# A hybrid decoder trunk on one Trainium2 core: its recurrence laid as one scheduling region, with a head's steps laid singly, POOL taking part of the DVE work, and the out weights split while the last head runs

## The chip, the cores and the metric

The kernel runs on one core of a Trainium2 chip. The core has a matrix engine (TensorE, here PE, with its weight loads as PEld), a vector engine (VectorE, DVE), an activation engine (ScalarE, ACT), a general engine (GpSimd, POOL) and an engine that only issues transfers here (SyncE, SP). Each runs its own instructions in the order in which they are laid, and waits for the others by semaphores. SBUF is the on-chip memory of 128 partitions; PSUM is the memory that matmuls write. The metric is the device time of one launch in microseconds.

## What is computed

The trunk has two layers on 1024 tokens of width 1024, all in fp32. Layer 0 mixes tokens with a gated linear recurrence, layer 1 with sliding-window attention; each layer has a gated FFN with a causal convolution of width 3. Only layer 0's mixer is touched by the change:

```python
def hgrn2_mixer(h, w_in, lower_bound, g_norm_w, w_out):
    q, f, i, g = jnp.split(h @ w_in, 4, axis=-1)
    lb = lower_bound.reshape(HG_HEADS, HG_DIM)          # 8 heads of 128
    fg = lb + (1.0 - lb) * jax.nn.sigmoid(heads(f))
    o = hgrn2_chunkwise(jax.nn.silu(heads(q)), 1.0 - fg, heads(i), jnp.log(fg))
    o = o * lax.rsqrt(jnp.mean(jnp.square(o), -1, keepdims=True) + RMS_EPS)
    o = o * g_norm_w * jax.nn.silu(heads(g))
    return o.reshape(B, S, D) @ w_out
# hgrn2_chunkwise: S_t = diag(f_t) S_{t-1} + k_t v_t^T ; o_t = S_t^T q_t
```

Then follow the residual, a layer norm, and the rest of the trunk.

## The kernel before

**Numbers in two parts.** An fp32 factor is held as a high part (a copy rounded to the matmul's type, made by ACT) and a low part (the rest, one DVE subtraction in `low_part`, L174). A product is three matmuls per block (`mm3`, L199 to L201): high x high, high x low, low x high. A matmul with a low part therefore waits for ACT and then for DVE.

**The x blocks (0 to 30 us).** x is loaded in eight blocks of 128 rows, transposed by PE into PSUM (`psax`), and stored as T (high and low) and, transposed but whole, as XS. For blocks 2 to 7 `turn_keep` makes T's high part (ACT, L226), T's low part from PSUM (DVE, L174), and the copy XS (ACT, L931). Between the transposes run the products for the i and g columns of head 0 (L838, L839). Then POOL or DVE adds quarters of XS (`sums_of`, L895): the sums are the moving factors of the fast matrix product below. Six small operations on the lower bounds of the gate (L976 to L986, DVE and ACT, with a table load L982) lie in between.

**Units and products.** f and q of head 0 are full products in two halves of the tokens, the second half first (L1628 to L1644). From head 1 on, the columns of a head are made by a scheme with seven products (numbered 1 to 7 in `product`) instead of eight, in 14 units, q and f, or i and g, of heads 1 to 7. Each product is 12 matmuls of 512 columns into one of four PSUM banks, with a factor of the weights in WR: seven rows of high and low parts, made from raw weights by ACT (L1303) and DVE (L174), with sums of quarters by DVE (L1567). What a bank holds is added up by ACT and DVE (L1392 to L1516) before its next product can start; this makes PE wait for DVE at L1416, L1470 or L1641, and for ACT at L1462.

**A head's recurrence** (`recur`, from L1058). It works by doubling: step i merges blocks of 2^i tokens. Ahead of step 0 DVE makes r0 = qs x kp (L1142), qp = qs x fg (L1144) and r1 = kp x qp (L1148). Each `update` (L1131, L1133, L1136) multiplies half of qp and kp by products of gates. PE makes the scores of each step from qp and kp (L205, 32 or 16 small matmuls for a step), and column sums with a matrix of ones. Of some steps a copy of qp and kp is stashed by ACT first (L1116, L1117). The scores land in the tiles A and Ab (128 x 1024 and 128 x 256). PE transposes kp, multiplies by the values V, DVE chains seven states St (L1220, L1222), PE adds A x V and St x qp, and `norm` (L1242 to L1268) squares on ACT, takes the power on POOL (L1244, L1245), scales on DVE, transposes on PE, and stores the head's rows to `yd`.

**What sets the order.** The class `Order` is a planner in Python that runs while the program is written. It keeps three clocks, od.t for PE, od.v for DVE and od.a for ACT, by fixed costs; generators (`spawn`) yield how long they wait, and `tick`, called after each group of matmuls, lays the steps that are due. Between steps it lays jobs (low parts and sums) from a list (`lay`, `lay_job`, `breathe`, `need`). All of it fixes only the order on each engine; on the chip the semaphores decide. The planner counts a matmul column at 1/2365 us. There are two regions with a hand-made order (`manual_schedule`): the x blocks up to head 0's i and g (PE, SP, ACT, DVE), and the rest up to the end of the out weights (these and POOL). Between them `conv_params` (L1028 to L1054) is a task of its own: it loads the FFN's convolution weights and the attention's bias, transposes them on PE into a `psax` buffer and copies them by DVE (L1039, L1051).

**The end (430 to 505 us).** The out projection multiplies the eight heads' rows by w_out. Heads 0 to 5 are read back from `yd` into WR (SP, L1681) and split into T (`move`, ACT L1610). w_out comes in halves: the first half is loaded once the last unit's job ("lo", last, 4) is done and cast by ACT at L1595, the second half is loaded later and cast at L1602 after the last head. The first passes with it (L1698) run between the scores of head 7, and the rows of x for the residual (Y, loaded at L337, used at L359) follow.

These are the two lines that the start's waits come from, and the loop of head 0's halves:

```python
                split(T[:, 0, :, ts], T[:, 1, :, ts], ps.rearrange("p (k t) -> p k t", k=KC))
                nc.scalar.copy(XS[:, tb, :], ps)
...
            for half in (1, 0):
                ts = slice(half * 512, (half + 1) * 512)
                for g in "fq":
                    ps = banks[half * 2 + (g == "q")]
```

Of the kernel before, what the change touches and what calls it, by code (L numbers as in the profile page):

```python
# [54 lines left out]
class Order:  # L55
# [5 lines left out]
    def __init__(self):  # L61
        self.t = 0.0
        self.v = 0.0
        self.a = 0.0
        self.fill = None
        self.chains = []
# [46 lines left out]
def trunk(ctx: ExitStack, tc: tile.TileContext, a: dict, out: bass.AP):  # L113
# [84 lines left out]
    def mm3(ps, st, mv, start, stop, n=512, more=False):  # L198
        nc.tensor.matmul(ps, st(0), mv(0), start=start, stop=False, skip_group_check=more)  # L199
        nc.tensor.matmul(ps, st(0), mv(1), start=False, stop=False, skip_group_check=more)  # L200
        nc.tensor.matmul(ps, st(1), mv(0), start=False, stop=stop, skip_group_check=more)  # L201
        od.t += 3 * n / 2365.0
# [505 lines left out]
    with tc.tile_pool(name="t", bufs=1, reuse_waits="tile") as raws, hgrn_pool as hp:  # L708
# [12 lines left out]
        values_in, values_done, keys_done, gates_read, queries_done = [[-1] for _ in range(5)]  # L721
# [159 lines left out]
        nc.gpsimd.memset(A, 0.0)  # L881
# [26 lines left out]

        with tc.tile_pool(name="ep", bufs=1, reuse_waits="tile") as ep:
# [15 lines left out]
            def turn_keep(tb):  # L925
# [4 lines left out]
                split(T[:, 0, :, ts], T[:, 1, :, ts], ps.rearrange("p (k t) -> p k t", k=KC))  # L930
                nc.scalar.copy(XS[:, tb, :], ps)  # L931

# [10 lines left out]
            with tc.manual_schedule(engines={EN.PE, EN.SP, EN.Activation, EN.DVE}):  # L943
# [63 lines left out]
                od.fill = lay  # L1007
                for tp, after in ((2, 2), (1, 6)):
# [4 lines left out]
                    if after == 2:  # L1013
                        for t in range(2):
                            sums_of(t, nc.gpsimd)
# [5 lines left out]
                for t in range(2, 4):  # L1021
                    sums_of(t, nc.vector)
                od.fill = None

        def conv_params():
            yield 330.0
            for l in range(2):
                crs = []  # L1028
                for k in range(2):
                    crs.append(hp.tile([88, P], F32, name="cr", bufs=2))  # L1030
                    for j in range(2):
                        q = 2 * k + j
                        src = a["ffn_conv_w"][l, q] if q < 3 else a["ffn_conv_b"][l]
                        nc.gpsimd.dma_start(crs[k][44 * j:44 * (j + 1), :], src.rearrange("(c p) -> c p", p=P))
                yield 10.0
                for k, cr in enumerate(crs):
                    ps = psax()
                    nc.tensor.transpose(ps[:, :88], cr, ident[:88, :88])
                    nc.vector.tensor_copy(cwt[:, l, 2 * k:2 * k + 2, :],  # L1039
                                          ps[:, :88].rearrange("p (a b) -> p a b", a=2))  # L1040
                    yield 3.0

            rb = hp.tile([88, P], F32, name="cr", bufs=2)[:32, :16]
            nc.gpsimd.dma_start(rb, a["rel_bias"])
            oh = hp.tile([32, 2 * P], F32, name="oh")
            nc.gpsimd.dma_start(oh, a["onehot"])
            yield 10.0
            ps = psax()
            nc.tensor.matmul(ps[:16, :2 * P], rb, oh, start=True, stop=True)
            rl = hp.tile([16, 2 * P], F32, name="oh")  # L1050
            nc.vector.tensor_scalar(rl, ps[:16, :2 * P], -1.0, None, op0=ALU.mult)  # L1051
            yield 3.0
            nc.gpsimd.dma_start(rbd, rl)

        params = od.spawn(conv_params())

        def recur(h, qs, fg, kp):
            qp = hp.tile([P, S], F32, name="qp")  # L1058
            tot = hp.tile([P, S], F32, name="tot")

# [62 lines left out]
            def update(i):  # L1123
# [3 lines left out]
                breathe()  # L1127
# [12 lines left out]
            yield 0.0  # L1140
            r0 = hp.tile([P, S], F32, name="St")
            nc.vector.tensor_tensor(r0, qs, kp, op=ALU.mult)  # L1142
            breathe()
            nc.vector.tensor_tensor(qp, qs, fg, op=ALU.mult)  # L1144
            od.vec(2.4)
            breathe()
# [3 lines left out]
            update(0)  # L1150
            gates_read[0] = h
            breathe()
# [5 lines left out]
            yield od.behind(-1.0, 5.0)  # L1158
            update(1)
            early = stash(2, fg if h else VT)  # L1160
            yield od.behind(0.0, 0.5)
            update(2)
# [11 lines left out]
            place(Ab, 0, chunks(sums0))  # L1174
            place(Ab[:, :, 1::2], 1, chunks(sums1), lambda t: t[:, 1::2])
            puts.pop(0)()
            update(4)
# [3 lines left out]
            for j in range(2):  # L1181
                dst = Ab.rearrange("p c (b u) -> p c b u", u=4)[:, :, :, 2:]
                place(dst, 2 + j, sums2[:, j * P:(j + 1) * P].rearrange("p (c b u) -> p c b u", c=NB, u=2), fours)
            yield wait
            pv = chunks(psax())
            low, high = scores(4, pv[:, :, :16], early, early), blocks(5, pv, kp, qp)
            update(5)
            early = stash(6, hp.tile([P, S], F32, name="kd"))
            low()
            update(6)  # L1190
# [7 lines left out]
            put = blocks(6, chunks(psax()), early, early)  # L1198
# [5 lines left out]
            put()  # L1204
            kd = hp.tile([P, S], F32, name="kd")
            nc.scalar.copy(kd, ps)
            od.act(1.0)
            keys_done[0] = h
            yield 2.2
# [3 lines left out]
            for c in range(NB - 1):  # L1213
                cs = slice(c * P, (c + 1) * P)
                mm32(ps[:, cs], kd[:, cs], V[:, c, :])
            St = hp.tile([P, NB, P], F32, name="St")
# [8 lines left out]
            yield od.behind(0.3, 2.6)  # L1225
# [9 lines left out]
        def norm(h, pv):  # L1235
# [11 lines left out]
            while gates_read[0] < min(h + 1, 1):  # L1247
                yield 0.2
            og = hp.tile([P, NB, P], F32, name="og")
# [51 lines left out]
        def cast(u, p, src):  # L1301
            w = WR[0][:, row_of(u, p), :]
            nc.scalar.copy(w[:, :512], src)  # L1303
            job(od.act(0.6), 0.61, lambda: low_part(w[:, 512:], src, w[:, :512], None), ("lo", u, p))
# [36 lines left out]
        def product(u, p):  # L1341
# [10 lines left out]
            for k in range(4):  # L1352
                mm3(ps, lambda j: w[:, 512 * j + P * k:512 * j + P * k + P], lambda j: moving(j, k),
                    p in (1, 5, 2) and k == 0, k == 3, more=p in (6, 7, 4, 3))
                od.tick()
            collect(u, p, ps)
# [25 lines left out]
        def keep_first(u, ps):  # L1382
# [6 lines left out]
            else:  # L1389
                while queries_done[0] < 0 or "asked" not in state[u - 1]:  # L1390
                    yield 0.2
# [4 lines left out]
        def keep(u, ps, cols):  # L1396
            kind, h = units[u]
            st = state[u]
            if kind == "q":
                while (queries_done if h > 1 else gates_read)[0] < h - 1:  # L1400
# [10 lines left out]
        def add_to(u, ps, cols, i):  # L1411
# [3 lines left out]
            yield 0.2  # L1415
# [29 lines left out]
        def first(u, i, ps, n):  # L1445
            kind, h = units[u]
            st, ts = state[u], slice(i * 512, (i + 1) * 512)
            if i == 0:

                def sum11():  # L1450
                    while "kept" not in st:
                        yield 0.2
                    yield 0.2
# [74 lines left out]
        def drive(cond):  # L1528
            for n in range(9999):
                if cond():  # L1530
                    return
                task = min((t for t in od.chains if t is not params), key=lambda t: t[0])
# [5 lines left out]

        def build_sums(go):
            for t in range(4):  # L1540
                for which in (7, 6):
                    split_sum(t, which)
                    yield 0.6
                a12, a22 = quarter(t, 1), quarter(t + 4, 1)
                job(od.t, 0.69, lambda a12=a12, a22=a22: nc.vector.scalar_tensor_tensor(
                    a12, a22, -1.0, a12, op0=ALU.mult, op1=sub), ("rows", t))
            left = {5: [0, 1, 2, 3], 3: [0, 1, 2, 3]}
# [551 lines left out]
```

## Time and profile before

| what | us |
|---|---|
| three runs: lowest, median, highest | 2137.88, 2137.92, 2140.2 |
| the profiled execution | 2138.2 |
| its span | 2136.4 |
| PE busy in the span | 2095.7 |
| DVE, ACT, POOL busy | 1797.0, 971.0, 271.7 |

The span runs from the first to the last instruction that the profiler shows; the execution's time has some 1.8 us around it. In rows of the profile a line of `kernel.py` stands with L, the arrow goes from the tiles read to the tile written (buffer numbers left out), and the times are in us unless marked ns. In a list of waits the row says who waited, for what, and then the total, the count and the longest. PEclk in a window is the mean share of full clock that the throttle granted to PE.

### The profile page before, as it was taken

The numbers are of one execution on the slowest core, as the hardware profiler recorded it, in microseconds if no ns is written. First come the engines' busy times: TensorE is split into PE (matmuls) and PEld (weight loads), VectorE is DVE, ScalarE is ACT, GpSimd is POOL, SyncE is SP. The second block draws the span as 40 slices with busy tenths as digits, with TensorE's granted clock in tenths as the row PEclk, the third lists the DMA queues.
The fourth block names the chain that finished last, engine by engine and source line by source line (L and its number), as shares of the span: only waits on it lengthen the run. The fifth ranks groups of instructions, "written<-read, shape, count | busy, mean of one in ns | idle before, by whom it ended". The sixth has DMA issues, their size and how long they took to land.

```text
span 2136.4 us, 31777 instructions
## 1 busy us (share of the span) xinstructions
PE 2095.7 (98%) x12303; PEld 1747.3 (82%) x12303; DVE 1797.0 (84%) x2453; ACT 971.0 (45%) x1570; POOL 271.7 (13%) x301
## 2 busy tenths in 40 slices
PE   8999999989999999999999999999999999999998
PEld 7788788767888888888888888888888888888887
DVE  5877777677999999987987858969999999978986
ACT  5555455442444444444433356743544444444430
POOL 2000000100121122100001112321031122000002
PEclk9999999999999999999999999999999999999999
DMA  4011111134235567737955601142255577549662
GB/s 162 21 51 50 50 50 50 45 130 147 90 119 175 165 162 162 164 107 246 316 166 174 178 23 44 27 144 94 79 182 177 149 166 160 132 151 323 224 216 97
DMA packets 241272, 286.82 MB, mean 134 GB/s; under 512 B 30121, under 2 KB 160081, under 8 KB 241121
## 3 DMA queue, kind: packets, MB, share of 16 engines
q1 hardware_dynamic: 221600, 235.11, 34.1%
q0 software_dynamic: 19232, 49.54, 10.8%
q8 instruction: 97, 1.59, 0.3%
q14 instruction: 55, 0.44, 0.1%
q10 hardware_dynamic: 288, 0.14, 0.0%
HBM read 241.72 MB, written 89.15 MB: 155 GB/s over the span
## 4 chain that ended last, share of the span: by engine, by line
PE 93%; DVE 3%; DMA 1%; ACT 1%; issue 1%; POOL 0%; SPq 0%; DVEq 0%; ACTq 0%; POOLq 0%
PE psmm L199 18%; PE psmm L201 18%; PE psmm L200 18%; PE psax L199 9%; PE psax L201 9%; PE psax L200 9%; PE psax L205 4%; PE psmm L209 1%; PE psmm L205 1%; PE psax L209 1%; PE psax L1873 1%; PE psmm L1698 1%; DMA raw<-in_hgrn_w_in_dram 1%; DVE WR L174 0%; DMA raw<-in_hgrn_w_out_dram 0%
## 5 line engine op out<-in xcount | busy, mean ns | idle before, releaser
L506 DVE SCALAR_TENSOR_TENSOR Y<-Y,cwt 128x1023 f32<-128x1023 f32 (+1 forms) x176 | 224.9, 1280 | 48.3 <-ACT Y L504 47.0
L226 ACT CAST HL<-rx 128x1024 fp32r<-128x1024 f32 (+1 forms) x151 | 150.6, 1006 | 155.9 <-PE psmm L200 25.9
L199 PE MATMUL psmm<-T,HL 128*128 128x512 f32 x512 | 200.6, 392 | 0.0
L201 PE MATMUL psmm<-T,HL 128*128 128x512 f32 x512 | 199.4, 389 | 0.0
L200 PE MATMUL psmm<-T,HL 128*128 128x512 f32 x512 | 199.3, 389 | 0.0
L174 DVE TENSOR_TENSOR HL<-rx,HL 128x1024 fp32r<-128x1024 f32 (+1 forms) x151 | 178.4, 1187 | 15.8 <-ACT HL L226 15.6
L504 ACT ACTIVATE Y<-Y,cwt 128x1024 f32<-128x1024 f32 x88 | 108.7, 1237 | 91.6 <-DVE Y L493 86.8
L248 POOL TENSOR_TENSOR rs<-rs,nhalf 128x1 f32<-128x1 f32 x32 | 45.3, 1416 | 726.7 <-DVE rs L247 726.7
L199 PE MATMUL psax<-T,HL 128*128 128x512 f32 x352 | 137.3, 390 | 0.0
L201 PE MATMUL psax<-T,HL 128*128 128x512 f32 x352 | 137.0, 389 | 0.0
L200 PE MATMUL psax<-T,HL 128*128 128x512 f32 x352 | 137.0, 389 | 0.0
L201 PEld LDWEIGHTS psmm<-T,HL 128*128 128x128 f32 x512 | 96.2, 188 | 20.1
L200 PEld LDWEIGHTS psmm<-T,HL 128*128 128x128 f32 x512 | 96.2, 188 | 19.5
L199 PEld LDWEIGHTS psmm<-T,HL 128*128 128x128 f32 x512 | 96.1, 188 | 19.6
L548 POOL COPY warm<-Y 128x1 f32<-128x1 f32 x64 | 65.1, 1018 | 354.4 <-DVE Y L487 349.7
L199 PE MATMUL psmm<-T,WR 128*128 128x512 f32 x224 | 91.5, 409 | 6.7 <-DVE qs L1641 4.2
L226 ACT CAST HT<-rx 128x1024 fp32r<-128x1024 f32 (+1 forms) x37 | 35.5, 960 | 130.8 <-DVE rx L461 62.3
L201 PE MATMUL psmm<-T,WR 128*128 128x512 f32 x224 | 88.8, 397 | 5.3 <-DVE WR L174 5.3
L200 PE MATMUL psmm<-T,WR 128*128 128x512 f32 x224 | 88.0, 393 | 0.0
L226 ACT CAST HL<-Y 128x1024 fp32r<-128x1024 f32 (+1 forms) x32 | 28.6, 892 | 116.8 <-DVE Y L461 41.0
L174 DVE TENSOR_TENSOR WR<-raw,WR 128x512 fp32r<-128x512 f32 x98 | 63.9, 685 | 21.0 <-ACT WR L1303 21.0
L201 PEld LDWEIGHTS psax<-T,HL 128*128 128x128 f32 x352 | 66.0, 188 | 13.8
(447 smaller groups left out, 5991.3 us busy)
## 6 DMA issues: line engine op xcount, KB each, us to landing
rx<-in_ffn_w_in_dram SPq DMA_DIRECT2D x136, 256.0 KB, 3.9
rx<-gd SPq DMA_DIRECT2D x118, 256.0 KB, 3.7
bsd<-in_ffn_w_out_dram POOLq DMA_DIRECT2D x36, 768.0 KB, 7.2
gd<-Y SPq DMA_DIRECT2D x44, 512.0 KB, 2.6
raw<-in_hgrn_w_in_dram SPq DMA_DIRECT2D x30, 512.0 KB, 5.0
rx<-in_ffn_w_out_dram SPq DMA_DIRECT2D x54, 256.0 KB, 4.4
R<-bsd SPq DMA_DIRECT2D x44, 256.0 KB, 5.1
Y<-in_ffn_w_in_dram SPq DMA_DIRECT2D x40, 256.0 KB, 4.1
```

Source lines behind the costliest of these rows:

```text
L174: make = lambda e: e.tensor_tensor(lo, src, hi.bitcast(F32), op=ALU.subtract)
L199: nc.tensor.matmul(ps, st(0), mv(0), start=start, stop=False, skip_group_check=more)
L200: nc.tensor.matmul(ps, st(0), mv(1), start=False, stop=False, skip_group_check=more)
L201: nc.tensor.matmul(ps, st(1), mv(0), start=False, stop=stop, skip_group_check=more)
L205: nc.tensor.matmul(ps, lhsT, rhs, start=start, stop=stop, **kw)
L209: nc.tensor.transpose(ps, src, ident)
L226: nc.scalar.copy(hi, src)
L248: nc.gpsimd.tensor_tensor(rs, rs, nhalf, op=ALU.pow)
L504: nc.scalar.activation(c, u, AF.Identity, bias=cwt[:, l, 3, ci:ci + 1], scale=cwt[:, l, 2, ci:ci + 1])
L506: nc.vector.scalar_tensor_tensor(c[:, sh:], u[:, :S - sh], cwt[:, l, 2 - sh, ci:ci + 1], c[:, sh:], op0=ALU.mult, op1=ALU.add)
L548: with tc.issue_after(nc.gpsimd.tensor_copy(tick, Y[:, 2 * (fc % 2) + (p == 4), :1]).ins):
L1698: nc.tensor.matmul(ps, T[:, x, kc, tb * P:(tb + 1) * P], us[kc][:, w, :], start=start and kc == 0, stop=False)
```

## The change

- **One region** from the x blocks to the out weights, with POOL's order made by hand in it too. The planner's rate goes from 2365 to 2260 columns per us in the second part.
- **XS and the sums.** ACT makes T's high part and XS in a row; DVE takes T's low part from XS in SBUF instead of PSUM. All twelve sums go to POOL (six were DVE's), and the splits of the sums start earlier.
- **Head 0's f and q**, the half laid last: q first into the first bank, f then into the second.
- **Steps of a head are laid singly.** `room()` lets each step wait until DVE's planned backlog is 1.6 us or less. r0 goes from DVE to POOL. The stash of step 2 goes into A, the score tile, so POOL clears A in every head; the buffers fg and VT that held it, and the list queries_done, are free of it. Scores of step 3 come before those of step 2 and before the column sums, blocks 5 before scores 4, the transposes of kp before blocks 6. The eight A x V products come first, then the seven St x qp.
- **Convolution and bias parameters** are loaded in heads 0 to 4, transposed into the last columns of the column sums' PSUM tile and copied by ACT.
- **Low parts of product 4** go to the front of the jobs and always press.
- **Out weights.** The loads of the first half start when ("lo", last - 1, 4) and ("lo", last, 4) are done; the casts are laid at planned landing times during the last unit, the second half is loaded and split inside the last head, and Y's loads come right behind it in SP's queue.

POOL's order from the sums to head 2. Before (XS are the sums, ss the norm's mean and power, yd the store of a head's rows):

```order
L895 TENSOR_TENSOR XS<-XS 128x512 x6
L1244 TENSOR_SCALAR ss<-ss 128x8
L1245 TENSOR_TENSOR ss<-ss,nhalf 128x8
L1274 DMA yd<-GV 128x1024
L1244 TENSOR_SCALAR ss<-ss 128x8
```

The same stretch now (St is the buffer that holds r0, A the score tile, cr the parameters):

```order
L902 TENSOR_TENSOR XS<-XS 128x512 x12
L1065 DMA cr<-in_ffn_conv_w_dram 44x128 x2
L1182 TENSOR_TENSOR St<-qs,kp 128x1024
L1212 MEMSET A 128x1024
L1065 DMA cr<-in_ffn_conv_w_dram 44x128
L1065 DMA cr<-in_ffn_conv_b_dram 44x128
L1182 TENSOR_TENSOR St<-og,kp 128x1024
L1290 TENSOR_SCALAR ss<-ss 128x8
L1291 TENSOR_TENSOR ss<-ss,nhalf 128x8
L1321 DMA yd<-GV 128x1024
```

Six sums, r0 of each head and a clearing of A have come to POOL; in heads 1 and 2 r0 stands ahead of the norm's power, in heads 3 and 6 behind it.

DVE's order in the last x blocks. Before (V and GV are head 0's values and gate, tot holds the f weights' low part for a while):

```order
L174 TENSOR_TENSOR T<-psax,T 128x8x128
L816 TENSOR_TENSOR GV<-GV,VT 128x256
L174 TENSOR_TENSOR T<-psax,T 128x8x128
L806 TENSOR_TENSOR V<-V,psmm 128x128
L806 TENSOR_TENSOR GV<-GV,psmm 128x128
L174 TENSOR_TENSOR tot<-raw_101,qp 128x1024
```

Now:

```order
L175 TENSOR_TENSOR T<-XS,T 128x8x128
L824 TENSOR_TENSOR GV<-GV,VT 128x256
L913 SCALAR_TENSOR_TENSOR HL<-XS,HL 128x4x128 x2
L175 TENSOR_TENSOR T<-XS,T 128x8x128
L814 TENSOR_TENSOR V<-V,psmm 128x128
L814 TENSOR_TENSOR GV<-GV,psmm 128x128
L924 SCALAR_TENSOR_TENSOR XS<-XS 128x512
L175 TENSOR_TENSOR tot<-raw_101,qp 128x1024
```

T's low part reads XS, two splits of sums have come between the last two blocks, and one more operation before the f weights' low part.

ACT's order while head 7 begins. Before (fg and qp, kp are the stash of step 2, HL the out weights, T<-WR the rows of earlier heads, VT and V the values of the last unit):

```order
L1116 COPY fg<-qp 128x128x4
L1117 COPY fg<-kp 128x128x4
L1595 CAST HL<-raw_99 128x1024
L1595 CAST HL<-raw_100 128x1024
L1595 CAST HL<-raw_101 128x1024
L1595 CAST HL<-raw_102 128x1024
L1610 CAST T<-WR 128x4x256 x2
L1462 COPY VT<-psmm 128x512
L1610 CAST T<-GV 128x256
L1514 COPY V<-psax 128x1024
```

Now:

```order
L1627 CAST HL<-raw_99 128x1024
L1627 CAST HL<-raw_100 128x1024
L1288 ACTIVATE sq,ss<-psax 128x128 x4
L1456 COPY GT<-psmm 128x512
L1627 CAST HL<-raw_101 128x1024
L1156 COPY A<-qp 128x128x4
L1157 COPY A<-kp 128x128x4
L1627 CAST HL<-raw_102 128x1024
L1509 COPY VT<-psmm 128x512
L1653 CAST T<-WR 128x4x256
L1561 COPY V<-psax 128x1024
```

The casts of the out weights have moved ahead and are spread between other work, and the copy VT no longer stands behind two moves of rows.

The diff, cut to what the prediction speaks of:

```diff
-        od.t += 3 * n / 2365.0
+        od.t += 3 * n / od.rate
...
+            if key[0] == "lo" and key[2] == 4:
+                return True
...
+        def room(us=1.6):
+            while od.v > od.t + us:
+                yield od.v - od.t - us
+            breathe()
...
-                split(T[:, 0, :, ts], T[:, 1, :, ts], ps.rearrange("p (k t) -> p k t", k=KC))
+                by_k = lambda t: t.rearrange("p (k t) -> p k t", k=KC)
+                nc.scalar.copy(T[:, 0, :, ts], by_k(ps))
                 nc.scalar.copy(XS[:, tb, :], ps)
+                low_part(T[:, 1, :, ts], by_k(XS[:, tb, :]), T[:, 0, :, ts], None)
...
+                for t in range(2, 4):
+                    sums_of(t, nc.gpsimd)
...
-                for t in range(2, 4):
-                    sums_of(t, nc.vector)
...
+            def turn(ps):
+                nc.tensor.transpose(ps[:, :88], cr, ident[:88, :88])
+                nc.scalar.copy(cwt[:, l, 2 * k:2 * k + 2, :], ps[:, :88].rearrange("p (a b) -> p a b", a=2))
+                od.act(0.3)
...
-            yield 0.0
+            yield from room()
             r0 = hp.tile([P, S], F32, name="St")
-            nc.vector.tensor_tensor(r0, qs, kp, op=ALU.mult)
-            breathe()
+            nc.gpsimd.tensor_tensor(r0, qs, kp, op=ALU.mult)
             nc.vector.tensor_tensor(qp, qs, fg, op=ALU.mult)
...
-            early = stash(2, fg if h else VT)
-            yield od.behind(0.0, 0.5)
-            update(2)
+            yield od.behind(-0.4, 0.0)
+            early = stash(2, flat(A))
+            yield max(od.a - od.t - 0.2, 0.0)
+            yield from update(2)
...
+            puts = [scores(3, chunks(ps[:, 768:896]), kp, qp), scores(2, chunks(ps[:, 384:512]), early, early)][::-1]
             column_sums(sums0, r0, 32)
             column_sums(sums1, r1, 16)
             column_sums(sums2, r2.rearrange("p j b u -> p (j b u)"), 16)
-            puts = [scores(2, chunks(ps[:, 384:512]), early, early), scores(3, chunks(ps[:, 768:896]), kp, qp)]
-            queries_done[0] = h
-            update(3)
+            if h < len(extras):
+                extras[h](ps[:, 896:])
+            nc.gpsimd.memset(A, 0.0)
+            yield from update(3)
...
             for c in range(NB):
                 cs = slice(c * P, (c + 1) * P)
-                mm32(ps[:, cs], A[:, c, :], V[:, c, :], stop=c == 0)
-                if c:
-                    mm32(ps[:, cs], qp[:, cs], St[:, c, :], start=False)
+                mm32(ps[:, cs], A[:, c, :], V[:, c, :], start=c % 4 == 0, stop=False, skip_group_check=True)
+            yield od.behind(0.3, 0.0)
+            for c in range(1, NB):
+                cs = slice(c * P, (c + 1) * P)
+                mm32(ps[:, cs], qp[:, cs], St[:, c, :], start=False, stop=c % 4 == 3, skip_group_check=True)
...
         def out_load():
-            while ("lo", last, 4) not in done_jobs:
-                yield 0.2
             for k in range(4):
+                freed = ("lo", last - 1 + k // 2, 4)
+                while freed not in done_jobs:
+                    yield 0.2
                 oraw.append(load4(out_loads(rows1, 0, (2 * k, 2 * k + 1))))
+                landing.append(max(od.t, laid_at[freed], landing[-1] - 5.5) + 6.7)
...
-                for g in "fq":
-                    ps = banks[half * 2 + (g == "q")]
+                for g in ("fq" if half else "qf"):
+                    n = 2 + (g == "q") if half else g == "f"
+                    ps = banks[n]
...
-            for u in range(4):
-                od.later(1.0 + 1.1 * u, lambda u=u: late_split(u))
+            od.spawn(late_splits())
+            drive(lambda: values_done[0] == NH - 1)
```

More of the change, by code (lines that the diff above doesn't have):

```diff
@@ L64, in __init__ @@
         self.a = 0.0
+        self.rate = 2365.0
         self.fill = None
@@ L907, in split_sum, with build_sums @@
                 ("x", which, t))
+        def build_sums(go, summed):
+            for t in range(4):
+                while t not in summed:
+                    yield 0.2
+                for which in (7, 6):
+                    split_sum(t, which)
+                    yield 0.6
+                a12, a22 = quarter(t, 1), quarter(t + 4, 1)
+                job(od.t, 0.69, lambda a12=a12, a22=a22: nc.vector.scalar_tensor_tensor(
+                    a12, a22, -1.0, a12, op0=ALU.mult, op1=sub), ("rows", t))
+            left = {5: [0, 1, 2, 3], 3: [0, 1, 2, 3]}
+            while left[5] or left[3]:
+                which = 5 if left[5] and (go or not left[3]) else 3
+                while which == 5 and not go:
+                    yield 0.2
+                t = left[which].pop(0)
+                while which == 3 and ("rows", t) not in done_jobs:
+                    yield 0.2
+                split_sum(t, which)
+                yield 0.6
         with tc.tile_pool(name="ep", bufs=1, reuse_waits="tile") as ep:
@@ L1537, in drive @@
             raise ValueError("the order never comes to its end")
[L1539 to L1547, printed above, removed]
-            while left[5] or left[3]:
-                which = 5 if left[5] and (go or not left[3]) else 3
-                while which == 5 and not go:
-                    yield 0.2
-                t = left[which].pop(0)
-                while which == 3 and ("rows", t) not in done_jobs:
-                    yield 0.2
-                split_sum(t, which)
-                yield 0.6
         prepared, WR, ring_pool = [], [], ExitStack()
@@ L1599, in late_split, with out_splits @@
-        def late_split(u):
-            both, parts = late_home(u, pair0)
-            src = lraw[u].rearrange("p (b n) -> p b n", b=2)
-            nc.scalar.copy(both[:, 0], src)
-            job(od.act(1.05), 1.14, lambda: low_part(both[:, 1], src, both[:, 0], None), ("late", u))
-            late.extend(parts)
+                landing.append(max(od.t, laid_at[freed], landing[-1] - 5.5) + 6.7)
+        def out_splits():
+            for u in range(4):
+                while u >= len(oraw) or (last, 6 if u < 2 else 7) not in ran or od.t < landing[u + 1]:
+                    yield 0.2
+                hl, raw = hl_at(u), oraw[u]
+                nc.scalar.copy(hl[:, 0], raw)
+                job(od.act(1.05), 1.22, lambda hl=hl, raw=raw: low_part(hl[:, 1], raw, hl[:, 0], None), ("out", u))
+                out_us.extend([hl[:, :, :512], hl[:, :, 512:]])
@@ new lines, in late_load, with late_splits @@
+        def late_load():
+            for u in range(4):
+                while ("out", u) not in done_jobs:
+                    yield 0.2
+                lraw.append(load4(out_loads(rows1, 1, (2 * u, 2 * u + 1))))
+                landing.append(max(od.t, laid_at["out", u], landing[-1] - 5.5) + 6.7)
+        def late_splits():
+            for u in range(4):
+                while u >= len(lraw) or od.t < landing[u + 5]:
+                    yield 0.2
+                both, parts = late_home(u, pair0)
+                src = lraw[u].rearrange("p (b n) -> p b n", b=2)
+                nc.scalar.copy(both[:, 0], src)
+                job(od.act(1.05), 1.14, lambda both=both, src=src: low_part(both[:, 1], src, both[:, 0], None), ("late", u))
+                late.extend(parts)
+                yield 0.6
@@ L1613, in moves @@
         def moves(h0, h1, tps):
-            while h0 == 6 and 6 not in turned:
+            while h0 == 6 and 6 not in turned or any(od.t < row_in[r] for r in range(h0, min(h1, 6))):
                 yield 0.2
```

187 lines of the change are left out of this document (93 added, 94 removed).

## The prediction

> **What bounds the kernel now.** I read the page first, for the busy shares, then the list of what TensorE (PE) waits for, then the windows with the granted clock, and last single records around each wait.
>
> ```profile
> span 2136.4 us, 31777 instructions
> PE 2095.7 (98%) x12303; PEld 1747.3 (82%) x12303; DVE 1797.0 (84%) x2453; ACT 971.0 (45%) x1570; POOL 271.7 (13%) x301
> ```
>
> PE is busy 98% of the span, so only its idle time and a slow clock can be won back. The waits of PE, in us in total, times and longest, are all in the part that the change touches, the first 505 us:
>
> ```profile
> PE psax L209 <- ACT VT L1462: 5.7, 2, 5.2
> PE psmm L201 <- DVE WR L174: 5.5, 4, 2.6
> PE psmm L199 <- DVE qs L1641: 4.2, 1, 4.2
> PE psax L209 <- DVE cwt L1039: 3.6, 1, 3.6
> PE psmm L199 <- DVE Y L359: 2.9, 1, 2.9
> PE psmm L1698 <- DVE HL L174: 1.8, 1, 1.8
> PE psax L209 <- ACT XS L931: 1.8, 2, 1.2
> PE psmm L869 <- DVE HL L850: 1.7, 1, 1.7
> PE psmm L199 <- DVE GT L1416: 1.5, 1, 1.5
> PE psmm L957 <- DVE XS L877: 1.0, 1, 1.0
> PE psmm L199 <- DVE fg L1416: 1.0, 1, 1.0
> PE psmm L839 <- DVE T L174: 0.8, 2, 0.4
> PE psax L205 <- DVE kp L1133: 0.5, 1, 0.5
> PE psmm L869 <- ACT HL L858: 0.4, 1, 0.4
> PE psmm L201 <- DVE tot L174: 0.3, 1, 0.3
> PE psax L205 <- ACT V L1514: 0.2, 1, 0.2
> ```
>
> They sum to 32.9 us. Three of them (L850, L877 and L858: 1.7 + 1.0 + 0.4 = 3.1) lie in the first 10 us, which the change leaves alone; 29.8 us are in its reach. The long ones cost more than their length. These windows give PE busy (x matmuls), PEclk, the granted clock, and DMA; the first is a stretch of products at full clock, 90 matmuls in 20 us or 0.22 us each, so 2.7 us for a product's 12:
>
> ```profile
> 45.00:65.00 20.00, 20.00 (x90) 1.00 0.19 53
> 20.00:30.00 10.00, 8.37 (x44) 0.83 0.35 106
> 70.00:80.00 10.00, 7.20 (x25) 0.83 0.00 0
> 260.00:270.00 10.00, 10.00 (x52) 0.83 0.00 0
> 400.00:410.00 10.00, 8.97 (x122) 0.66 0.03 6
> 450.00:460.00 10.00, 8.01 (x240) 0.83 0.04 13
> 500.00:510.00 10.00, 7.10 (x25) 0.83 0.83 317
> ```
>
> Each follows one wait: the x blocks' at 22 to 24 us, L1641, the longest L174 (2.6), L1039, L1462, L359. A mean of 0.83 over 10 us is 1.7 us lost, 0.66 is 3.4: 5 x 1.7 + 3.4 = 11.9, of which I count 11, since a little falls on idle time. No wait up to 1.8 us alone has such a window, every one from 2.6 us on has. The profiled execution took 2138.2 us (1.8 around its span), 0.3 over the median, so the sum may be read against either. With all in reach gone it would be 2138.2 - 29.8 - 11 = 2097.4.
>
> [...]
>
> **Part by part: what goes.** *q before f in head 0's second half* (L1641): the wait was for the DVE multiply behind eight low and sum operations; laid first, it has f's 24 matmuls (5.4 us) ahead of its reader. -4.2 - 1.7. *Conv parameters* in the sums' PSUM tile with copies on ACT (L1039): nothing else waits for these, and the tile's own readers stand before its next user. -3.6 - 3.4. *Low parts by the p4 rule and the rate of 2260* (the four L174): counted along the new order, each stands one to three products ahead of its matmuls. -5.5 - 1.7. *The end* (L1462, L359, HL L174, kp, V):
>
> ```profile
> 450.84 0.58 ACT L1462 COPY VT<-psmm 128x512 f32<-128x512 f32 x1
> 495.89 4.63 DVE L174 TENSOR_TENSOR TX<-raw,TX 128x1024 fp32r<-128x1024 f32 x4 [0.53 <-ACT TX L1602]
> 504.47 0.69 DVE L359 SCALAR_TENSOR_TENSOR Y<-Y,psmm 128x512 f32<-128x512 f32 x1 [0.16 <-DMA Y<-in_x_dram]
> ```
>
> ACT's copy came behind four casts in its queue that wait for out weights; now these are loaded from the second last unit on and two casts stand behind the copies of the products. The late split (TX, 4.63 us) ran after the last head and kept the Y load back; now it runs inside the head. -11.1 - 3.3. I put 1.4 us in their place: 0.5 where the last transposes have three matmuls of cover, 0.9 where Y's first rows still land after their reader is due. The rest of the list (x blocks 2.9 with 1.7 of clock, L1416 2.5) goes too and is priced anew below: what takes its place is the point of this forecast.
>
> **What is added: POOL beside DVE.** POOL gets r0 = qs x kp in every head (DVE before), and six more 128x512 sums of x in the start. What such work does to DVE is in the trace:
>
> ```profile
> 616.40 2.40 POOL L511 TENSOR_TENSOR Y<-Y 128x1024 f32<-128x1024 f32 x1 [44.79 <-DVE Y L506]
> 616.70 2.65 DVE L462 TENSOR_TENSOR rx<-rx,Y 128x512 f32<-128x512 f32 x1
> L462 DVE TENSOR_TENSOR rx<-rx,rx 128x512 f32<-128x512 f32 x24 | 16.4, 684 | 0.0
> 624.24 2.39 POOL L511 TENSOR_TENSOR Y<-Y 128x1024 f32<-128x1024 f32 x1 [2.39 <-DVE Y L506]
> 624.59 3.13 DVE L174 TENSOR_TENSOR HL<-rx,HL 128x1024 fp32r<-128x1024 f32 x1
> 18.28 4.03 POOL L895 TENSOR_TENSOR XS<-XS 128x512 f32<-128x512 f32 x3 [7.95 <-ACT XS L931]
> 18.35 1.24 DVE L983 TENSOR_TENSOR lm<-le 128x8 f32<-128x8 f32 x1 [0.57 <-ACT le L981]
> 21.07 1.22 DVE L174 TENSOR_TENSOR T<-psax,T 128x1024 fp32r<-128x1024 f32 x1
> ```
>
> The DVE operation at 616.70 ends 0.55 after POOL's end and takes 2.65 us where its group takes 0.68; the 128x8 one at 18.35 ends with POOL's first sum. The last row, with one input in PSUM, runs beside POOL in its usual 1.22. So a DVE operation that reads two SBUF tiles stands still while POOL reads SBUF. [...]
>
> ```profile
> L1142 DVE TENSOR_TENSOR St<-qs,kp 128x1024 f32<-128x1024 f32 x7 | 8.6, 1222 | 0.2
> L1148 DVE TENSOR_TENSOR r<-kp,qp 128x512 f32<-128x512 f32 x8 | 5.5, 692 | 0.3
> 17.19 1.01 ACT L931 COPY XS<-psax 128x1024 f32<-128x1024 f32 x1 [1.29 <-DVE T L174]
> 18.33 1.28 ACT L982 ACT_TABLE_LOAD   x1
> ```
>
> *r0, every head.* r0 and DVE's first step qp = qs x fg are released by the same matmul. [...] So moving 1.22 us (L1142) off DVE costs its chain 2.3 us there instead of 0: bounds 0 (ports free) and 2.4, taken at 2.3 since both 1024-wide rows above are held to POOL's end. What a head can absorb, counted along the new order from that matmul to the next scores, products at 2.7 us against the DVE rows laid up to its kp update: head 0 13.7 against 13.3, head 1 14.6 against 14.2, head 2 14.5 against 13.8, head 4 18.0 against 15.9, head 5 17.9 against 15.6, head 7 a bank's reader with 0.7 to spare (its product at 12.3). With 2.3 more the stalls are about 1.9, 1.9, 1.6, 0.2, 0, 1.6. In heads 3 and 6 POOL comes to r0 only after the norm's power; DVE's kp update waits, with 20 us and more of products as cover: 0 and 0.4. Sum 7.6, all below 2.6 a piece, so no slow clock. The memset of A, now in each head, only writes, and its tile is next used a dozen us later: 0.
>
> *The start.* T's low part now reads the copy XS instead of PSUM: it starts a copy (1.0, L931) later, and it has become a two-SBUF operation. The 1.29 us that ACT waited between its copies goes. But XS is complete at 16.9 and not 18.2, so POOL's sums start before the small gate-bound operations L1010 to L1017, which then alternate with 1.3 us sums; ACT's exp, table load (1.28) and next T cast stand behind them. Without blocking T's low part at 22 us comes 1.9 us late, with one to two sums 3 to 4.2: taken 3.1, with 1.7 of clock. The last block's low part is laid behind three two-SBUF operations and so alternates with four sums, 5.2 us: it is due near 40 us and comes near 43.6, 3.6 late (0 without blocking), with 1.2 of clock (7 in 10 of 1.7). The f weights' low part behind it: 0.9. Sum 10.5 in place of 2.9 + 1.7.
>
> *The rest.* room() lays the steps of a head singly; the new rows leave DVE no more work than it had. Scores 3 before 2, V x A apart from St x qp: no new wait that I find. I allow 2.1 us for stalls that a count by hand misses.
>
> Sum: 2138.2 - 29.8 - 11 + 1.4 + 7.6 + 10.5 + 2.1 = **2119.0 us**.
>
> **Rivals.** *POOL and DVE don't get in each other's way here*, because the waits fall so that POOL works beside PSUM readers: heads 1.5, start 2.5, the rest as above: 2138.2 - 40.8 + 1.4 + 1.5 + 2.5 + 2.1 = 2105. Against it stand the rows above. Chance 0.17. *The four stalls of 1.6 to 1.9 pass 2.6 us* through a late neighbour in DVE's queue and each gets a slow window: 4 x (1.0 + 1.7) = 10.8 more, 2130. Chance 0.15. *The out weights come late anyway*: SP has the five WR rows queued behind the weight loads, and ACT's copy of V in head 7 stands behind a cast of such a row; the wait L1462 and its clock stay, +7: 2126. Chance 0.08. *Slower*: r0 sets the pace of every head. If the heads that I give slack have none, because the planner's own backlog limit lays DVE steps as late as PE allows, each of 8 heads loses 2.3 and falls into the slow clock for 1.7: 32 instead of 7.6, 2143. It decides from (19.2 + 7.6) / 8 = 3.4 us a head. Against it: heads 3 to 6 have over 2 us of cover by count. Chance 0.07.
>
> **The numbers.** The forecast itself has 0.53. The range runs from the first rival, 2103 with its own small misses, to the second, 2131; it leaves out the slower case and tails, some 0.15. Faster by over 0.2% (4.3 us, about what a measurement of this kernel can tell from no change) is all but the last rival and a little: 0.89; within 0.03; slower 0.08.
>
> **What would show it.** Right: no wait on L1641's or L1039's successors; DVE's r1 or its neighbour at 2.5 to 3 us beside POOL's r0 in most heads; two waits of PE of 2 us or more on T between 20 and 45 us, with windows below 1.00; waits of 1 to 2 us at the scores of heads 0, 1, 2 and 7; no slow window from 60 to 440. Wrong: r1 at its 0.69 beside POOL (then 2105), any slow window inside a head, or a wait of ACT for in_hgrn_w_out as long as before.

## The result

The changed kernel takes 2111.23 us in the median (2110.27 to 2111.84, four runs) against 2138.89 (2137.88 to 2140.2, four runs): ratio 0.987, 95% interval 0.9853 to 0.9887. The forecast was 2119.0, the range 2103 to 2131. It is 27.7 us faster, where 19 were forecast, and 7.8 us better than the forecast.

The page of the profiled execution (2110.27 us):

```profile
span 2108.5 us, 31814 instructions
PE 2087.6 (99%) x12305; PEld 1741.4 (83%) x12305; DVE 1803.3 (86%) x2434; ACT 972.5 (46%) x1576; POOL 317.3 (15%) x323
```

All that PE waits for now, in the same columns as before (total, times, longest):

```profile
PE psmm L847 <- DVE T L175: 4.9, 2, 3.2
PE psmm L200 <- DVE GT L1464: 1.6, 2, 1.1
PE psmm L846 <- ACT T L959: 1.5, 1, 1.5
PE psax L206 <- DVE kp L1173: 1.2, 1, 1.2
PE psmm L989 <- DVE XS L885: 1.0, 1, 1.0
PE psmm L200 <- DVE Y L360: 0.5, 1, 0.5
PE psmm L877 <- DVE HL L858: 0.5, 1, 0.5
PE psax L206 <- ACT V L1561: 0.5, 2, 0.2
PE psmm L877 <- ACT HL L866: 0.4, 1, 0.4
PE psmm L200 <- ACT fg L1456: 0.4, 1, 0.4
PE psmm L200 <- ACT T L227: 0.3, 1, 0.3
```

They sum to 12.8 us, 32.9 before (the list leaves out gaps under 0.15 us, 0.3 in all). The long waits of the middle and the end are gone (WR's low parts, the convolution parameters, the copy VT); half of what is left is in the x blocks. Two windows (PE busy, matmuls, PEclk, DMA share and GB/s): the first holds the only slow clock that is left while PE works, the second stood at 0.66 before:

```profile
40.00:50.00 10.00, 7.32 (x29) 0.83 0.19 52
400.00:410.00 10.00, 10.00 (x86) 1.00 0.58 185
```

**POOL beside DVE in a head.** POOL's r0 and, on DVE, qp and r1 of head 2, single records:

```profile
161.32 3.45 POOL L1182 TENSOR_TENSOR St<-qs,kp 128x1024 f32<-128x1024 f32 x1 [27.81 <-PE psax L206]
```
```profile
161.27 1.23 DVE L1183 TENSOR_TENSOR qp<-qs,fg 128x1024 f32<-128x1024 f32 x1 [1.04 <-PE psax L206]
162.53 2.79 DVE L1187 TENSOR_TENSOR r<-kp,qp 128x512 f32<-128x512 f32 x1
```

DVE starts 0.05 us earlier and runs undisturbed (1.23 us); r0's record is 3.45 us long instead of the 2.38 of head 6, since it waits for qp's end; then r1 stands until r0 ends and takes 2.79 instead of 0.69. Over all heads r1's group is

```profile
L1187 DVE TENSOR_TENSOR r<-kp,qp 128x512 f32<-128x512 f32 x8 | 15.9, 1987 | 0.3
L1183 DVE TENSOR_TENSOR qp<-qs,fg 128x1024 f32<-128x1024 f32 x7 | 10.8, 1540 | 3.9 <-PE psax L206 3.9
```

against 5.5 and 8.5 us before: 10.4 and 2.3 us more, where r0 itself had cost DVE 9.8 (8.6 and 1.2 for its two groups). In head 4 a low part stands between qp and r1, and it is the one that stands still (2.90 us instead of 0.69). The transfer of r0 has cost DVE more than it took away: 14.9 us against 9.8.

**The x blocks.** ACT (the exp and T's cast), DVE (two splits of sums, T's low part) and POOL (four sums in one row), three answers:

```profile
20.43 0.22 ACT L1013 ACTIVATE le<-le 128x16 f32<-128x16 f32 x1 [3.85 <-DVE le L1012]
20.67 1.28 ACT L1014 ACT_TABLE_LOAD   x1
21.96 0.20 ACT L1014 ACTIVATE warm<-nhalf 128x1 f32<-128x1 f32 x1
22.07 0.99 ACT L959 CAST T<-psax 128x1024 fp32r<-128x1024 f32 x1
```
```profile
36.96 3.47 DVE L913 SCALAR_TENSOR_TENSOR HL<-XS,HL 128x512 fp32r<-128x512 f32 x2
40.35 2.28 DVE L175 TENSOR_TENSOR T<-XS,T 128x1024 fp32r<-128x1024 f32 x1
```
```profile
34.41 7.14 POOL L902 TENSOR_TENSOR XS<-XS 128x512 f32<-128x512 f32 x4 [3.40 <-ACT XS L960]
```

ACT waits 3.85 us for a DVE operation on 128x8 elements that stands behind sums, and T's cast comes behind it at 22.07, for which PE waits 1.5 us. The two splits take 3.47 us instead of 1.28, T's low part 2.28 instead of 1.22; it ends at 42.6, where the working had 43.6.

### The profile page after: what moved, and what is told of

Read it like the earlier page. It is cut to its first block, busy times and chain, and to the rows that moved or that the text cites. A ratio compares the mean times of both kernels' runs of the same rounds, so it can differ in the third digit from the quotient of the medians.

```text
span 2108.5 us, 31814 instructions
## 1 busy us (share of the span) xinstructions
PE 2087.6 (99%) x12305; PEld 1741.4 (83%) x12305; DVE 1803.3 (86%) x2434; ACT 972.5 (46%) x1576; POOL 317.3 (15%) x323
## 3 DMA queue, kind: packets, MB, share of 16 engines
q8 instruction: 97, 1.59, 0.3%
## 4 chain that ended last, share of the span: by engine, by line
PE 94%; DVE 4%; issue 1%; ACT 1%; DMA 0%; SPq 0%; DVEq 0%; ACTq 0%
PE psmm L200 18%; PE psmm L202 18%; PE psmm L201 18%; PE psax L200 10%; PE psax L201 10%; PE psax L202 10%; PE psax L206 4%; PE psmm L206 1%; PE psmm L210 1%; PE psax L1916 1%; PE psax L210 1%; PE psmm L1743 1%; DVE T L175 0%; DVE r L1187 0%; DVE Y L261 0%
## 5 line engine op out<-in xcount | busy, mean ns | idle before, releaser
L202 PEld LDWEIGHTS psax<-T,HL 128*128 128x128 f32 x352 | 66.1, 188 | 13.8
L200 PEld LDWEIGHTS psax<-T,HL 128*128 128x128 f32 x352 | 66.1, 188 | 13.6
```

## Experiments

Each edit is to the changed kernel, but for the last one, to the kernel before. The medians stand beside 2111.23 of the changed kernel; the ratio is to the kernel before. Only the kernel before was run again beside each group of edits; its medians were 2138.0 to 2138.9, so a difference of 1 us between two edits says nothing. "Shared port" in the expectations is my name for what the rows show, DVE operations on two SBUF tiles standing still beside POOL (2.79 us instead of 0.69); by what path the two engines reach SBUF no run shows.

**r0 on DVE.**

```diff
-            nc.gpsimd.tensor_tensor(r0, qs, kp, op=ALU.mult)
+            nc.vector.tensor_tensor(r0, qs, kp, op=ALU.mult)
             nc.vector.tensor_tensor(qp, qs, fg, op=ALU.mult)
-            od.vec(1.2)
+            od.vec(2.4)
```

> The changed kernel (2111.2 us) with r0 = qs x kp back on DVE, one DVE operation of 1.22 us ahead of qp. Theory of the shared port: beside POOL's r0 DVE's r1 took 2.7 to 2.8 us instead of 0.69, 2.1 more, so putting r0 back costs DVE 1.2 and wins 2.1; the waits inside the heads (3.8 us in all) fall by one to two us: 2109 to 2111. Rival, POOL as relief: DVE has 1.2 us more to do in each of 8 heads and the waits rise by 4 to 8: 2115 to 2119.

Measured 2112.55 (2110.07 to 2114.53), ratio 0.9878 (0.9864 to 0.9893): no gain, which fits neither number. The waits in the heads are gone but for 0.6 us, yet a new one stands at the end:

```profile
PE psmm L200 <- DVE Y L360: 5.1, 1, 5.1
```

Its profiled execution also has six slow steps of the clock (last section) against one, four of them in the x blocks, which the edit doesn't touch. The planner was told of the 1.2 us and moved one late split behind the last transposes and one weight load ahead of Y in SP's queue. So this run changed two things, and the next one keeps the order.

**r0 on DVE, order kept** (the same edit without that of od.vec).

> The changed kernel with r0 on DVE and the planner not told of it, so that PE, ACT and SP keep their order row for row. Shared port: the head waits (3.8 us) go and nothing else moves: 2107 to 2108. Rival, POOL as relief: 1.2 us more for DVE in each head, 2115 to 2119.

2107.86 (2107.77 to 2111.34), ratio 0.9862 (0.9849 to 0.9875). r0 and r1 on DVE:

```profile
L1182 DVE TENSOR_TENSOR St<-qs,kp 128x1024 f32<-128x1024 f32 x7 | 8.6, 1223 | 4.7 <-PE psax L206 3.9 <-ACT kp L1680 0.8
L1187 DVE TENSOR_TENSOR r<-kp,qp 128x512 f32<-128x512 f32 x8 | 5.5, 691 | 0.2
```

r1 is back at 0.69, and of the 3.8 us of waits in the heads 1.8 are gone (L1464 but for 0.2, half of the wait for fg). The 1.2 us at the scores of head 0 stay: with r0 on DVE its chain is 0.9 us shorter but must wait for kp, 0.8 us later than fg. The median moved by 3.4, about what the first theory predicts, three of the four runs being at 2107.8 and one at 2111.3. The heads give less than that: PE lays the same matmuls in the same order in both kernels, and set side by side they gain 2.3 us between 80 and 430 us. The two profiled executions differ by 2.5 us with one slow step each; 0.8 of it comes in the first 8 us, ahead of all that was edited, and 1.2 are lost again at 532 us, where PE waits for L413. POOL as relief, 2115 to 2119, is out.

**r0 made twice by POOL**, the opposite edit.

```diff
             nc.gpsimd.tensor_tensor(r0, qs, kp, op=ALU.mult)
+            nc.gpsimd.tensor_tensor(r0, qs, kp, op=ALU.mult)
```

> The changed kernel with r0 made twice by POOL in each head, one behind the other. Shared port: DVE's steps lose up to 2.4 us more a head, all of it at heads 0, 1 and 7, which wait already, the excess over 1 to 2 us of slack at the others: 8 to 15 us more, 2119 to 2126, with slow windows if waits pass 2.6 us. Rival, POOL has time to spare in the heads: 2111 to 2113.

2127.26 (2126.29 to 2128.63), ratio 0.995 (0.9933 to 0.9967): 16 us more, over the upper end of 15. The waits of the heads (line numbers are one higher):

```profile
PE psmm L200 <- DVE GT L1465: 5.8, 2, 3.2
PE psmm L200 <- ACT fg L1457: 2.7, 1, 2.7
PE psmm L200 <- DVE GV L1465: 2.3, 2, 1.1
```

The second r0 stops DVE's next step behind r1, the first update of qp (5.6 us for the eight of the changed kernel):

```profile
L1171 DVE TENSOR_TENSOR qp<-qp,fg 128x512 f32<-128x512 f32 x8 | 15.9, 1990 | 0.2
```

DVE's own work is the same in all three kernels but for r0, and PE waits nowhere for POOL itself. What a head waits for follows the time in which POOL reads: the cause is shown by taking it away and by doubling it.

**T's low part from PSUM**, at its place in every queue.

```diff
-                low_part(T[:, 1, :, ts], by_k(XS[:, tb, :]), T[:, 0, :, ts], None)
+                low_part(T[:, 1, :, ts], by_k(ps), T[:, 0, :, ts], None)
```

> The changed kernel with T's low part read from PSUM again, its place in every queue unchanged. Shared port: the low part of the last x block takes 1.22 instead of 2.28 us, since only one input is in SBUF; the wait of 3.2 us falls to about 2.1 and the slow window may go: 2108.5 to 2110. Rival, only the longer queue ahead of it counts: 2111.

2107.78 (2106.45 to 2108.65), ratio 0.9856 (0.9841 to 0.9871).

```profile
PE psmm L847 <- DVE T L175: 2.9, 2, 1.7
```

The last block's low part, and POOL's six sums beside it:

```profile
39.25 1.21 DVE L175 TENSOR_TENSOR T<-psax,T 128x1024 fp32r<-128x1024 f32 x1
```
```profile
34.33 9.20 POOL L902 TENSOR_TENSOR XS<-XS 128x512 f32<-128x512 f32 x6 [7.71 <-ACT XS L960]
```

The longer of these two waits, 3.2 us, is 1.2 now, nearly twice the step of 1.1 expected: the low part takes 1.1 us less and starts 1.1 earlier, since an operation on GV ahead of it (L824, 1.52 us in the changed kernel) takes 0.49 now that POOL's first sum runs beside the low part of the block before and not behind it. PE's wait for T's cast by ACT fell from 1.5 to 0.6. T's low part begins behind the copy XS in this run too, so an earlier start by its new input is not the cause. One input in PSUM was enough here to run beside POOL (1.21 us, 2.28 with both inputs in SBUF). The matmuls set side by side gain 2.1 us in the x blocks, of the 3.4 of the median.

**The six sums on DVE.**

```diff
-                for t in range(2, 4):
-                    sums_of(t, nc.gpsimd)
                 first_split("f", ("qp", "tot"))
...
                 nc.vector.tensor_copy(msk, mf)
+                for t in range(2, 4):
+                    sums_of(t, nc.vector)
```

> The changed kernel with the six sums of x blocks 2 and 3 back on DVE, behind the masks as before the change. Shared port: nothing of POOL runs beside the last x block any more, its low part is not late, PE's wait of 3.2 us at 42.7 us and the slow window behind it (1.7) go: 2106 to 2107. Rival: DVE's 3.7 us more make the sums late for head 0, and a wait comes back ahead of its first products: 2111 to 2115.

2109.06 (2107.84 to 2110.38), ratio 0.9863 (0.9848 to 0.9878). The wait of 3.2 us went, as expected, and the rival's came, with the one slow step behind it (77.3 us instead of 43.7):

```profile
PE psmm L200 <- ACT fg L1456: 2.4, 1, 2.4
```

Both theories were half right: without POOL's sums T's low part is in time, and DVE has no 3.7 us to spare for them ahead of head 0.

**Together.** r0 (order kept) and T from PSUM:

> The former, and T's low part from PSUM. If the two costs are separate they add: 3.8 of the heads and 3.4 of the start, 2103.5 to 2104.5. If the start's gain only moves the wait into head 0: 2106 to 2108.

2104.26 (2102.99 to 2106.1), ratio 0.9842 (0.9828 to 0.9855): 7.0 us under the changed kernel, 3.4 and 3.4 added. All its runs lie below all of the changed kernel's; the two intervals overlap by a hair. The matmuls set side by side add up too, to less: r0 gains 2.6 us in the heads on top of T from PSUM, and T 2.1 in the x blocks on top of r0; the rest of the 7.0 is not shown to be these edits' doing, since the start, the clock and the wait for L413 vary by as much. With the sums on DVE as well:

> The former, and the six sums of blocks 2 and 3 on DVE: nothing of the change is left on POOL but the clearing of A. The two waits on T and tot that remain there (1.2 and 0.8) go: 2101.5 to 2102.5. Rival: DVE's 3.7 us bring the wait for ACT's copy fg (2.4 us in the run with the sums alone): 2104 to 2106.

2105.6 (2104.42 to 2106.33), ratio 0.9847 (0.9834 to 0.986): nothing won over the former, and the rival's wait (1.9 us for fg) is there. r0 on POOL and T from XS don't pay here. Where the six sums should be is open: on DVE they are 2.2 us better in the changed kernel and 1.3 worse here, and in both cases the intervals overlap.

**f first again in head 0's last half.**

```diff
-                for g in ("fq" if half else "qf"):
-                    n = 2 + (g == "q") if half else g == "f"
+                for g in "fq":
+                    n = 2 * half + (g == "q")
```

> The changed kernel with f before q again in the last half of head 0. By the prediction's term the wait for the DVE multiply comes back with its slow window, 4.2 + 1.7: 2117. Rival: the splits of the sums are laid earlier now and DVE is not behind there, so the order of the two doesn't matter: 2111 to 2112.

2111.2 (2109.12 to 2112.42), ratio 0.9873 (0.9859 to 0.9886): no difference, the rival's number. DVE's multiply is at the same time as before the change, and the first product of the first unit begins 5.6 us later (71.38, 65.76 before):

```profile
72.20 0.69 DVE L1686 TENSOR_TENSOR qs<-qs,psmm 128x512 f32<-128x512 f32 x1
```
```profile
71.38 0.39 PE L200 MATMUL psmm<-T,WR 128*128 128x512 f32 x1
```

So the rival was right in the time and wrong in its reason: DVE is not earlier, PE comes later, held up by the x blocks. In this execution that is mostly clock: up to there PE has four slow steps against one before the change, 5.1 us, and 1.6 us more of waits (1.1 us are won elsewhere). The wait that the swap was to save had been paid at the start. Whether the swap pays in a kernel with a short start wasn't tried.

**Out weights loaded late.**

```diff
-                freed = ("lo", last - 1 + k // 2, 4)
+                freed = ("lo", last, 4)
```

> The changed kernel with all four loads of the out weights' first half behind the last unit's low part of product 4, as before the change. By the prediction ACT then stands at casts that wait for loads and its copy of V in head 7 comes late: 5 to 7 us more, 2116 to 2118. Rival, what counts is where the casts are laid, by landing times, and not when the loads start: 2111 to 2112.5.

2112.55 (2110.13 to 2113.24), ratio 0.9875 (0.9861 to 0.989): the upper end of the rival's range. No wait for the copy of V's unit came back. One row of the end is new:

```profile
PE psax L206 <- DVE GV L1315: 1.0, 1, 1.0
```

**Steps not laid singly.**

```diff
         def room(us=1.6):
-            while od.v > od.t + us:
-                yield od.v - od.t - us
             breathe()
+            return
+            yield 0.0
```

> The changed kernel without the limit on DVE's planned backlog: a head's steps are laid as soon as they are due, several at once. If laying them singly matters, low parts come late behind them and waits of PE on WR return: 2116 to 2122. Rival, the limit only moves steps inside DVE's slack: 2110 to 2113.

2119.74 (2118.68 to 2120.41), ratio 0.9911 (0.9896 to 0.9925): 8.5 us more, as the first theory has it. But the waits are not on WR's low parts; a bank's reader (L1464) and Y stand behind the bunched steps:

```profile
PE psmm L200 <- DVE GT L1464: 4.7, 2, 4.0
PE psmm L200 <- DVE Y L360: 3.3, 1, 3.3
```

Not all of the 8.5 us need be the steps' doing. The profiled execution has five slow steps of the clock against one; two lie behind the wait of 4.0 us, but three lie in the x blocks, which the edit leaves alone, and two more there cost 3.4 us.

**The old rate and the old rule for product 4.**

```diff
-            if key[0] == "lo" and key[2] == 4:
-                return True
...
-            jobs.insert(0 if p == 4 else len(jobs), (od.act(0.6), 0.61, ...
+            jobs.insert(len(jobs), (od.act(0.6), 0.61, ...
...
-            od.fill, od.rate = lay, 2260.0
+            od.fill, od.rate = lay, 2365.0
```

> The changed kernel with the planner's old rate of 2365 columns per us and the old rule for the low parts of product 4. By the prediction's term the four waits on WR's low parts and a slow window come back: 5.5 + 1.7, 2117 to 2119. Rival, room() and the shorter queue keep the low parts in time by themselves: 2111 to 2113.

2114.88 (2113.34 to 2115.49), ratio 0.9887 (0.9872 to 0.9902): 3.7 us more, between the two. One wait on a low part is back, and two others:

```profile
PE psax L206 <- issue: 1.6, 1, 1.6
PE psax L206 <- DVE GT L1313: 1.2, 1, 1.2
PE psmm L202 <- DVE WR L175: 1.1, 1, 1.1
```

Here too the profiled execution has three slow steps in the x blocks against one, so of the 3.7 us only the part that these waits explain is the edit's for certain.

**The kernel before, with the parameters copied by ACT.**

```diff
-                    nc.vector.tensor_copy(cwt[:, l, 2 * k:2 * k + 2, :],
+                    nc.scalar.copy(cwt[:, l, 2 * k:2 * k + 2, :],
```

> The kernel before, with the convolution parameters copied out of PSUM by ACT instead of DVE, and nothing else. If DVE's late copies hold the PSUM buffer, the wait of 3.6 us and the slow window behind it (3.4) go: 2131. Rival, the two buffers taken out of turn hold the scores whichever engine copies: 2135 to 2138.

2132.04 (2131.53 to 2134.01) against 2138.82 for the kernel before, run beside it, ratio 0.997 (0.9958 to 0.9983).

```profile
PE psax L209 <- ACT cwt L1039: 0.5, 1, 0.5
```

3.6 us became 0.5, and the time fell by 6.8 where 7.0 were expected. This one engine in one line is a quarter of the whole gain. In the profiled execution (2133.01) the two slow steps at 400 us are gone, but the slow steps fell from seven to six in all, since other waits lie differently on the clock's grid (last section); so the agreement to 0.2 us is in part luck.

## Why the prediction held, and where its terms were off

By stage, in us, the terms that the prediction set in place of the old waits, and what the profile after has (unseen: gaps under 0.15 us outside the heads):

| stage | forecast | measured |
|---|---|---|
| first 10 us | 3.1 | 1.9 |
| x blocks, with slow clock | 10.5 | 6.4 + 1.7 |
| heads | 7.6 | 3.8 |
| end | 1.4 | 0.8 |
| unseen | 2.1 | 0.1 |
| sum | 24.7 | 14.7 |

The difference of 10 us is that between 2119.0 and the profiled 2110.3, to 1.3 that I can't place. The forecast's signs held in part: of the two waits of 2 us or more on T one came (3.2 us, the other is 1.7), and of the waits of 1 to 2 us at the scores of heads 0, 1, 2 and 7 those of heads 0 (1.6) and 7 (1.4).

- **What goes.** Right for the stretch of the convolution parameters, by experiment, and in the sum for the end and the low parts: none of these waits is left. Two reasons are not shown. That the swap of q and f removes the wait L1641 fell with f_first; that the out weights' early loads remove L1462 fell with out_late, and the laying of their casts among the last unit's copies is what remains, which no run took apart. For the low parts the rate and the rule are worth 3.7 us at most, about half of the term of 7.2.
- **POOL beside DVE.** The step that decided the forecast was right in what it foresaw: r1 at 2.7 to 2.8 us beside r0 in heads 0 to 3 and 7 (a neighbour in heads 4 and 5; in head 6 r0 comes late as foreseen, and DVE's update of kp waits 3.2 us for it; in head 3 it was foreseen late and wasn't), two waits over 1.6 us on T's parts, and the first rival, 2105, is out. The 2.3 us a head rested on two rows of the kernel before, and in both POOL is ahead of DVE. That in a head DVE's qp goes first and r1 then waits for POOL's r0 was my estimate; the run shows it in head 2 (qp 1.23 us, r1 2.79) and the other way round in head 5 (qp 3.43, r1 0.69). The memset of A costs DVE nothing, as assumed: two operations beside it at 85.78 take 0.69 us each, as elsewhere. The term that was mis-sized is that of the heads, double the truth: 3.8 instead of 7.6, with 0.7 at head 1 instead of 1.9 and 0.1 at head 2 instead of 1.6. Less still is r0's alone: putting it back on DVE won 2.3 us there. A likely reason, which no run separates, is that I counted each DVE operation at its record (0.69 us) and not at its spacing in a row (0.6 in head 0, where they start at 74.47, 75.08 and 75.68), so the slack was larger than counted.
- **The clock.** The step "no wait up to 1.8 us has a slow window, every one from 2.6 us on has" failed; see the last section. Of the two slow stretches taken for the start (1.7 and 1.2) one came, and r0_dve, with the same instructions up to there, had four.
- **Laying steps singly** was given no term at all, "the new rows leave DVE no more work". It is worth 5 to 8.5 us by no_room (the lower end without the clock's chance in the x blocks), a fifth to a third of the gain. Without it the changed kernel came out at the forecast (2119.74), for another reason; so the hit owes something to luck, one term left out against others taken too large.

## What to carry to other kernels

Before work is moved from DVE to POOL, see what DVE runs beside it: here an operation with two SBUF inputs stood still for POOL's whole read (0.69 us became 2.79), so a 1.2 us operation moved away cost its neighbours 1.9, and one input in PSUM was enough to run beside it (1.21 us). An undo run must keep the order of the other engines (a planner that is told of the new cost moves other things), or it measures two changes. And a wait that disappears was not always removed by the edit meant for it: undo the edits one at a time before crediting them.

## What was not expected of the hardware

**The slow clock comes on a grid.** In the traces the slow stretches of a run, while PE works, lie on one grid of 3.41 us and last one or two steps of it: in the kernel before they begin at 24.62, 72.41, 260.14, 400.09, 451.29 and 505.90, the later ones 14, 69, 110, 125 and 141 steps from the first; in r0_dve's x blocks slow steps begin at 24.34, 27.75, 44.82 and 48.23, the later ones 1, 6 and 7 steps from the first. What counts in these rows is how much of one step PE was busy, and so where a wait falls on the grid. The same wait of 2.6 us on a WR low part at 260 us, in windows of one step (PE busy, matmuls, PEclk, DMA share and GB/s), first in the kernel before, then in before_conv_act:

```profile
256.73:260.14 3.41, 0.83 (x4) 1.00 0.04 12
260.14:263.55 3.41, 3.41 (x16) 0.50 0.00 0
```
```profile
254.93:258.34 3.41, 2.66 (x12) 1.00 0.69 206
258.34:261.76 3.42, 1.59 (x13) 1.00 0.01 4
261.76:265.17 3.41, 3.41 (x27) 1.00 0.00 0
```

Inside one step it leaves 0.83 us of work and the next step runs at half clock (0.50); across two it leaves 2.66 and 1.59 and nothing follows. The x blocks' waits of 1.5 and 1.7 us, first in the changed kernel, then in r0_dve, whose instructions are the same up to there:

```profile
23.19:26.60 3.41, 1.73 (x11) 1.00 0.06 18
26.60:30.01 3.41, 3.41 (x21) 1.00 0.00 0
```
```profile
20.93:24.34 3.41, 1.64 (x11) 1.00 0.71 214
24.34:27.75 3.41, 1.99 (x10) 0.50 0.00 0
27.75:31.17 3.42, 3.42 (x13) 0.50 0.00 0
```

No slow step in the one, two in the other, 3.4 us apart for the same work. Counted over all fourteen traces, every step at full clock with less than 1.45 us of work (37 of them) is followed by a slow one, 8 of the 17 with 1.45 to 1.8 us, and none of the 8548 with more (in the traces of the kernel before and the changed one alone 6 of 6, 1 of 4 and none of 1221); a step that is already slow was followed by another with up to 2.75 us of its slower work (2.64 in r0_dve, at 44.82). Between 1.45 and 1.8 both happened, so PE's busy time in a step does not settle it alone; what else does was not shown. This chance is in every time here: r0_dve's four runs spread over 4.5 us, at granted clocks of 0.994 to 0.997, and differences of 3 us between kernels with waits of 1.5 us and more are to be read with the list of waits beside them.

**Who goes first.** In head 2, released by the same matmul, DVE started 0.05 us ahead of POOL and was not slowed (qp 1.23 us); POOL's r0 came next, although DVE's next operation, r1, was due 0.03 us after qp, and r1 took 2.79 us instead of 0.69. In head 5 POOL was ahead by 0.22 us, and it was DVE's qp that stood still, for POOL's whole operation (1.22 us became 3.43):

```profile
312.60 2.58 POOL L1182 TENSOR_TENSOR St<-qs,kp 128x1024 f32<-128x1024 f32 x1 [27.82 <-PE psax L206]
```
```profile
312.82 3.43 DVE L1183 TENSOR_TENSOR qp<-qs,fg 128x1024 f32<-128x1024 f32 x1
```

In these rows the two take turns, operation by operation; so too beside POOL's sums (1.29 us each in the kernel before), where two DVE splits took 3.47 us instead of 1.28.
